# Encoder layer on one Trainium2 core: in the first feed-forward's second run, partial sums reach x by ScalarE and accumulating DMAs instead of VectorE

## The chip, the cores and the metric

The kernel runs on one core of one Trainium2 chip. The time is device microseconds of one execution. TensorE (PE in the profile) does the matmuls, ScalarE (ACT) and VectorE (DVE) the elementwise work, GpSimd (POOL) little here, and SyncE (SP) issues nearly all DMAs. PE writes its results to PSUM, eight banks of 128 x 512 f32; everything else lies in SBUF, 128 partitions wide. Each engine runs its own instructions strictly in order and waits on semaphores for the others.

## The reference, cut to what matters

One layer of an encoder, with the same weights, for two batches: a prompt of 1024 tokens and a sample of 256 tokens, model width 1024, feed-forward width 2816, all in f32:

```
x <- LN1(alpha*x + 0.5*SwiGLU_1(x))                      # the first FFN: the change is here
x <- LN2(alpha*x + W_out[ RMS(S5(x)) ; RMS(Hyena(x)) ])
x <- LN3(alpha*x + 0.5*SwiGLU_2(x))
SwiGLU(x) = (silu(x @ w_gate) * (x @ w_up)) @ w_down
```

S5 is a state-space scan that the kernel does with matmuls against tables; the tables are made from the weights on the chip. Hyena is a long convolution.

## The kernel before, in words

Each f32 matmul is done as three: both operands are split into a high part and a rest (`split`, L171 on ScalarE and L172 on VectorE), and high x high, high x rest and rest x high are summed in PSUM.

The first FFN is run twice, each time as a generator `ffn`: run `fa` takes four tiles of 128 tokens (the sample and the first two of the prompt), run `fb` the other six of the prompt. A run goes through the feed-forward width in 22 columns of 128 (`ft`). For each, `gate_up` makes gate and up in four PSUM banks (L298), silu (L306, ScalarE) and the product (L307, VectorE) give the hidden values, and these are split. Down is done for groups of columns: eighteen columns make nine groups of two, and the last four make the tenth group. For one group, `down` goes over the token tiles and over the two halves of the model width: six matmuls (L331; twelve in the last group) make one 128 x 512 partial sum in one of only two banks (`bd`), and VectorE adds it to the residual x in SBUF: L336 in the first group, which also multiplies x by alpha, L338 in all others. In `fb`, which has six tiles, a group is thus a block of 12 partial sums and 72 matmuls. After the last group's sum each tile is normalised (L239 to L245) and stored. A bank is free for the next partial sum but one when its sum has been read out.

Alongside `fb`, `weave` emits pieces of another generator, `prep`, which makes S5's tables: first in eight steps of many small VectorE operations (L421 to L426), three ScalarE operations each (L558, L561) and eight stores that ScalarE issues (L564); then 32 steps with small transposes and matmuls on PE (L589, L611, L623, L628), ScalarE copies out of PSUM (L612 and others) and stores on SP's queue (L613, L620, L637).

The generators only emit operations. A building layer fixes the order on each engine when the program is built, by priority and by a model of when each operation could start, and puts in the semaphore waits; on the chip this order stands.

Of the kernel before, what the change touches and what calls it, by code (L numbers as in the profile page):

```python
# [13 lines left out]
ALU = mybir.AluOpType  # L14
# [154 lines left out]
def split(K, src, hi, lo):  # L169

    K.nc.scalar.activation(out=hi, in_=src, func=AF.Copy)  # L171
    K.nc.vector.tensor_tensor(out=lo, in0=src, in1=hi.bitcast(F32), op=ALU.subtract)  # L172
# [37 lines left out]
def chunks_of(T):  # L210
    return [(o, min(512, T - o)) for o in range(0, T, 512)]
# [21 lines left out]
def layer_norm(K, x, g, b, eps, parts=1, done=None):  # L233

    V = K.nc.vector
    st = K.small.get()[:, 0:12].rearrange("p (a b) -> p a b", a=2)
    mv = K.small.get()
    for i in range(2):
        V.bn_stats(out=st[:, i], in_=x[:, i * 512:(i + 1) * 512])  # L239
    V.bn_aggr(out=mv[:, 0:2], in_=st)  # L240
    rsqrt(K, mv[:, 2:3], mv[:, 1:2], 1.0, eps)
    for i in range(parts):
        c = slice(i * (1024 // parts), (i + 1) * (1024 // parts))
        V.scalar_tensor_tensor(out=x[:, c], in0=x[:, c], scalar=mv[:, 0:1], in1=g[:, c], op0=ALU.subtract, op1=ALU.mult)
        V.scalar_tensor_tensor(out=x[:, c], in0=x[:, c], scalar=mv[:, 2:3], in1=b[:, c], op0=ALU.mult, op1=ALU.add)  # L245
        if done:
            done(c)


def load_row(K, dst, row):  # L250
    K.nc.sync.dma_start(out=dst, in_=row.partition_broadcast(128))


def ffn(K, NT, x, xT, wg, wu, wd, lng, lnb, cfg, done):


    nc = K.nc
    T = NT * 128
    unit, size = cfg.get("unit", 1), cfg.get("size", 2)
    chunks = chunks_of(T)  # L260
    fw = cfg.get("raw", 256)
    raw = K.ring(2, 8, fw)
    wgu = K.ring(cfg.get("wgu", 2), 2, 8, 128, dt=F32R)
    bg = Banks(K, cfg["bg"])
    bd = Banks(K, cfg["bd"])
    rawgu, rawdn, ready = {}, {}, {}
    lnv, extras = [], []

    def extra(*dims):
        extras.append(K.newr(*dims))  # L270
        return extras[-1].v

    def weights(i):

        ft, up = divmod(i, 2)
        if ft >= NFT or i in ready:
            return
        o = ft * 128 % fw
        if o == 0:
            r = raw.get()  # L280
            nc.sync.dma_start(out=r, in_=(wg, wu)[up][:, ft * 128:ft * 128 + fw].rearrange("(dt p) f -> p dt f", p=128))
            rawgu[up] = r
        ready[i] = w = wgu.get()
        with K.tc.high_priority(offset=cfg.get("ahead", 0)):
            split(K, rawgu[up][:, :, o:o + 128], w[:, 0], w[:, 1])

    def gate_up(ft):
        pss = []
        for i in (2 * ft, 2 * ft + 1):
            weights(i)  # L290
            weights(i + 1)
            w = ready.pop(i)
            pss.append([bg.get(n) for _, n in chunks])
            todo = [(d, wv, c, k) for d in range(8) for wv, ks in ((0, (0, 1)), (1, (0,))) for c in range(len(chunks)) for k in ks]
            if ft == 0:
                todo.sort(key=lambda t: t[2])
            for d, wv, c, k in todo:
                nc.tensor.matmul(pss[-1][c], lhsT=w[:, wv, d], rhs=xT.parts[k][c].at(d),  # L298
                                 start=(d == 0 and wv == 0 and k == 0), stop=(d == 7 and wv == 1))
        if ft == NFT - 1:  # L300
            raw.free()
        hv = [h.get() for h in hr] if ft < NFT - 4 + size + 1 else [extra(2, n) for _, n in chunks]
        with K.tc.high_priority(offset=cfg.get("hp", 0)):
            for c, (_, n) in enumerate(chunks):
                h = tmp.get()[:, 0:n]
                nc.scalar.activation(out=h, in_=pss[0][c], func=AF.Silu)  # L306
                nc.vector.scalar_tensor_tensor(out=h, in0=pss[1][c], scalar=0.5, in1=h, op0=ALU.mult, op1=ALU.mult)  # L307
                split(K, h, hv[c][:, 0], hv[c][:, 1])
        return hv

    def load_down(ft):
        if ft < NFT:
            rawdn[ft] = rawd.get()
            nc.sync.dma_start(out=rawdn[ft], in_=wd[ft * 128:(ft + 1) * 128, :])

    def wdown(ft):
        r = rawdn.pop(ft)
        w = wdn.get() if ft < NFT - 4 + size else extra(2, D)
        with K.tc.high_priority(offset=cfg.get("ahead", 0)):
            split(K, r, w[:, 0], w[:, 1])  # L320
        load_down(ft + len(rawd.bufs))
        return w

    def down(grp, ws, last):
        for s in range(NT):
            for dh in range(2):
                ps = bd.get(512)
                n = 0
                for h, w in zip([hs[f] for f in grp], ws):
                    for a, b in ((0, 0), (0, 1), (1, 0)):  # L330
                        nc.tensor.matmul(ps, lhsT=h[s // 4][:, a, s % 4 * 128:(s % 4 + 1) * 128], rhs=w[:, b, dh * 512:(dh + 1) * 512],  # L331
                                         start=(n == 0), stop=(n == 3 * len(grp) - 1))
                        n += 1
                xv = x.at(s)[:, dh * 512:(dh + 1) * 512]
                if grp[0] == 0:
                    nc.vector.scalar_tensor_tensor(out=xv, in0=xv, scalar=ALPHA, in1=ps, op0=ALU.mult, op1=ALU.add)  # L336
                else:
                    nc.vector.tensor_tensor(out=xv, in0=ps, in1=xv, op=ALU.add)  # L338
            if last:
                cut = cfg.get("cut") if s == NT - 1 else None  # L340
                layer_norm(K, x.at(s), lnv[0].v[:, 0], lnv[0].v[:, 1], LN_EPS, *((2, cut) if cut else ()))
                if not cut:
                    done(s)


    starts = list(range(0, NFT - 4, size))
    groups = [tuple(range(f, min(f + size, NFT - 4))) for f in starts] + [tuple(range(NFT - 4, NFT))]
    weights(0)
    yield 0.01
    rawd = K.ring(cfg.get("rawd", 1), D)  # L350
    wdn = K.ring(size, 2, D, dt=F32R)
    hr = [K.ring(size + 1, 2, n, dt=F32R) for _, n in chunks]
    tmp = K.ring(2, chunks[0][1])
    hs = {0: gate_up(0)}
    for f in range(len(rawd.bufs)):
        load_down(f)
    yield unit
    for n, grp in enumerate(groups):
        last = n == len(groups) - 1
        for f in grp:  # L360
            if f not in hs:
                hs[f] = gate_up(f)
                yield unit
        if last:
            xT.free()
            wgu.free()
            lnv.append(K.new(2, D))
            load_row(K, lnv[0].v[:, 0], lng)
            load_row(K, lnv[0].v[:, 1], lnb)
        ws = [wdown(f) for f in grp]  # L370
        if last and "tail" in cfg:
            cfg["tail"]()
        if not last:
            hs[grp[-1] + 1] = gate_up(grp[-1] + 1)
            yield unit
        down(grp, ws, last)
        yield unit * len(grp) / 2
    for b in [lnv[0], rawd, wdn, tmp] + hr + extras:
        b.free()


# [1169 lines left out]
def emit(ctx, tc, nc, A, dbg=None):  # L1551
    K = Ctx(ctx, tc, nc)
# [27 lines left out]
    def load_x(tiles):  # L1580
        x = Parts(K, len(tiles), D)
        for i, (src, s) in enumerate(tiles):
            nc.sync.dma_start(out=x.at(i), in_=src[:, s])
        return x

    def tokens(ap, nm):
        return ap.rearrange("(c s) d -> c s d", s=PARTS[nm][1])
# [7 lines left out]
    def ffn1(tiles, cfg, done=None):  # L1595

        x = load_x([(tokens(A["x_" + nm][0], nm), s) for nm, s in tiles])

        def each(i):
            nm, s = tiles[i]  # L1600
            nc.sync.dma_start(out=scr["x1_" + nm][:, s], in_=x.at(i))
            if done:
                done(x, i)

        xT = transposed(x, len(tiles), cfg["bd"])
        yield from ffn(K, len(tiles), x, xT, g("ffn1_w_gate"), g("ffn1_w_up"), g("ffn1_w_down"), g("ln1_g"), g("ln1_b"), cfg, each)
        x.free()
# [6 lines left out]
    keep, out, x1T = {}, {}, {}  # L1614
# [16 lines left out]

    fb = ffn1([("prompt", s) for s in range(2, 8)], dict(bg=(0, 1, 2, 3), bd=(4, 5), tail=to_mix, rawd=2), turn1)
    fa = ffn1([("sample", 0), ("sample", 1), ("prompt", 0), ("prompt", 1)],
              dict(bg=(0, 1), bd=(2, 3), raw=128, tail=lambda: steps(fb, 1)))
    steps(fa, 1)
# [252 lines left out]
```

## Time and profile before

| | us |
|---|---|
| median of 3 runs (lowest, highest) | 2579.18 (2578.24, 2588.45) |
| the profiled execution | 2584.32 |
| its span, first to last instruction | 2582.5 |
| PE busy | 2523.1 (98%) |
| DVE busy | 1810.0 (70%) |
| ACT busy | 812.3 (31%) |
| POOL busy | 74.7 (3%) |

All times in the rows below are of the profiled execution, counted from the start of its span. A row of a group of instructions gives their count, the busy time, the mean of one, and the idle time of the engine just before them with what ended it. ACTq and SPq are the sequencers of ScalarE and SyncE issuing DMAs. `s` is any SBUF buffer of the pool, `banks` is PSUM, `cst` a constant.

### The profile page before, as it was taken

The page shows a single profiled execution, that of the slowest core. Times are in us where ns is not written, and L with a number is a line of the kernel's source. Part 1 is how long each engine was busy: PE and PEld are TensorE (multiplying, and loading weights), DVE is VectorE, ACT ScalarE, POOL GpSimd, SP SyncE. Part 2 cuts the span into 40 slices and gives each one's busy share as a digit, 9 for nine tenths or more (in the row PEclk, how much of TensorE's full clock was granted, in tenths as well). Part 3 has the DMA queues.
Part 4 walks back from the last instruction along what each step waited for, and adds up shares of the span by engine and source line. Part 5 has one row for each costly group of instructions (what it writes and reads, how often), then busy time and mean ns, then how long its engine had stood idle before and what let it go on. Part 6 is the DMA issues. An engine that isn't in the chain of part 4 may idle for free.

```text
span 2582.5 us, 32676 instructions
## 1 busy us (share of the span) xinstructions
PE 2523.1 (98%) x12833; PEld 2112.1 (82%) x12833; DVE 1810.0 (70%) x3016; ACT 812.3 (31%) x1218; POOL 74.7 (3%) x58
## 2 busy tenths in 40 slices
PE   8999999999999999999999999999989999999998
PEld 6767887888888888788888878898768888888887
DVE  6777777568944666557896888788886556556437
ACT  5443344321322222223444313333332222223200
POOL 0000000000000000000000000000230000000001
PEclk9999999999999999999999999999999999999999
DMA  6332333533632333355566754564432223245311
GB/s 198 117 88 83 106 102 98 171 103 110 166 86 75 109 100 104 87 156 146 170 179 180 237 189 145 168 189 151 141 114 90 89 74 98 74 143 191 124 40 65
DMA packets 329073, 326.44 MB, mean 126 GB/s; under 512 B 41068, under 2 KB 285445, under 8 KB 328150
## 3 DMA queue, kind: packets, MB, share of 16 engines
q1 hardware_dynamic: 293366, 305.99, 37.5%
q10 hardware_dynamic: 35552, 18.36, 2.7%
q8 instruction: 101, 1.65, 0.3%
q14 instruction: 54, 0.44, 0.1%
HBM read 249.57 MB, written 74.46 MB: 125 GB/s over the span
## 4 chain that ended last, share of the span: by engine, by line
PE 82%; DVE 12%; DMA 3%; issue 2%; POOL 1%; ACT 1%; SPq 0%; DVEq 0%; ACTq 0%; POOLq 0%
PE banks L298 26%; PE banks L1367 16%; PE banks L331 12%; PE banks L1510 8%; PE banks L857 4%; PE banks L1238 3%; DVE s L927 3%; PE banks L774 3%; PE banks L1060 2%; DVE s L172 2%; PE banks L1201 1%; DVE s L245 1%; PE banks L1113 1%; DVE s L975 1%; DMA s<-in_ffn_w_gate_dram 1%
## 5 line engine op out<-in xcount | busy, mean ns | idle before, releaser
L298 PE MATMUL banks<-s,s 128*128 128x512 f32 (+1 forms) x4224 | 792.8, 342 | 3.3 <-ACT s L171 2.5
L298 PEld LDWEIGHTS banks<-s,s 128*128 128x128 f32 x4224 | 650.4, 190 | 99.6 <-issue 10.7
L171 ACT ACTIVATE s<-s 128x1024 fp32r<-128x1024 f32 (+3 forms) x467 | 437.8, 955 | 860.7 <-PE banks L298 239.0
L172 DVE TENSOR_TENSOR s<-s,s 128x1024 fp32r<-128x1024 f32 (+3 forms) x467 | 505.1, 1096 | 193.2 <-ACT s L171 191.0
L1367 PE MATMUL banks<-s,s 128*128 128x512 f32 x1848 | 423.4, 391 | 4.3 <-DVE s L172 3.4
L1367 PEld LDWEIGHTS banks<-s,s 128*128 128x128 f32 x1848 | 347.5, 188 | 78.7 <-DVE s L172 4.9
L331 PE MATMUL banks<-s,s 128*128 128x512 f32 x1584 | 393.0, 396 | 2.0 <-DVE s L172 1.0
L331 PEld LDWEIGHTS banks<-s,s 128*128 128x128 f32 x1584 | 291.2, 189 | 64.2 <-issue 2.1
L857 PE MATMUL banks<-s,s 128*128 128x512 f32 (+1 forms) x1152 | 238.1, 361 | 0.0
L1510 PE MATMUL banks<-s,s 128*128 128x512 f32 x704 | 216.8, 389 | 0.2 <-DVE s L172 0.2
L857 PEld LDWEIGHTS banks<-s,s 128*128 128x128 f32 x1152 | 188.3, 190 | 28.1 <-DVE s L172 0.4
L338 DVE TENSOR_TENSOR s<-banks,s 128x512 f32<-128x512 f32 x204 | 139.1, 688 | 49.1 <-PE banks L331 48.0
L1510 PEld LDWEIGHTS banks<-s,s 128*128 128x128 f32 x704 | 132.1, 188 | 28.1 <-DVE s L172 0.7
L1383 DVE TENSOR_TENSOR s<-banks,s 128x512 f32<-128x512 f32 x110 | 75.9, 690 | 106.5 <-PE banks L1367 105.7
L1510 PE MATMUL banks<-s 128*128 128x512 f32 x352 | 136.9, 389 | 0.0
L1238 PE MATMUL banks<-s,s 128*128 128x512 f32 x480 | 125.2, 409 | 3.2 <-ACT s L171 1.6
L1516 DVE TENSOR_TENSOR s<-banks,s 128x512 f32<-128x512 f32 x80 | 55.0, 690 | 97.1 <-PE banks L1510 97.1
L230 POOL TENSOR_TENSOR cst<-cst 128x1 f32<-128x1 f32 (+2 forms) x38 | 49.9, 1313 | 2496.0 <-DVE cst L229 2496.0
L1238 PEld LDWEIGHTS banks<-s,s 128*128 128x128 f32 x480 | 90.1, 192 | 23.1 <-ACT s L171 2.0
L307 DVE SCALAR_TENSOR_TENSOR s<-banks,s 128x512 f32<-128x512 f32 (+1 forms) x88 | 47.6, 554 | 84.3 <-PE banks L298 83.4
L543 DVE TENSOR_TENSOR s<-s,cst 128x288 f32<-128x288 f32 (+1 forms) x128 | 53.5, 438 | 53.5 <-PE banks L623 26.9
L676 DVE TENSOR_TENSOR s<-banks,s 128x512 f32<-128x512 f32 (+2 forms) x112 | 59.2, 552 | 44.4 <-ACT s L793 20.4
(210 smaller groups left out, 2347.8 us busy)
## 6 DMA issues: line engine op xcount, KB each, us to landing
s<-in_ffn_w_down_dram SPq DMA_DIRECT2D x88, 512.0 KB
s<-in_ffn_w_gate_dram SPq DMA_DIRECT2D x66, 512.0 KB
s<-in_ffn_w_up_dram SPq DMA_DIRECT2D x66, 512.0 KB
s<-in_ffn_w_gate_dram SPq DMA_DIRECT2D x11, 1024.0 KB
s<-in_ffn_w_up_dram SPq DMA_DIRECT2D x11, 1024.0 KB
scr_h<-s SPq DMA_DIRECT2D x22, 512.0 KB
s<-scr_h SPq DMA_DIRECT2D x22, 512.0 KB
scr_tab<-s ACTq DMA_DIRECT2D x64, 160.0 KB
```

Of the source, the lines that this page charges most:

```text
L171: K.nc.scalar.activation(out=hi, in_=src, func=AF.Copy)
L172: K.nc.vector.tensor_tensor(out=lo, in0=src, in1=hi.bitcast(F32), op=ALU.subtract)
L298: nc.tensor.matmul(pss[-1][c], lhsT=w[:, wv, d], rhs=xT.parts[k][c].at(d), start=(d == 0 and wv == 0 and k == 0), stop=(d == 7 and wv == 1))
L331: nc.tensor.matmul(ps, lhsT=h[s // 4][:, a, s % 4 * 128:(s % 4 + 1) * 128], rhs=w[:, b, dh * 512:(dh + 1) * 512], start=(n == 0), stop=(n ...
L338: nc.vector.tensor_tensor(out=xv, in0=ps, in1=xv, op=ALU.add)
L774: nc.tensor.matmul(ps, lhsT=F[kt][a].v[:, s, i], rhs=b.v[:, s], start=(n == 0), stop=(n == 3 * NT // R - 1))
L857: nc.tensor.matmul(p, lhsT=w[:, wv, d], rhs=xT[nm].parts[k][c].at(d), start=(d == 0 and wv == 0 and k == 0), stop=(d == 7 and wv == 1))
L927: TT = lambda o, a, b, op: V.tensor_tensor(out=o, in0=a, in1=b, op=op)
L1238: nc.tensor.matmul(ps, lhsT=y[s // per][a].v[:, k, ts], rhs=W[k].v[:, b, dh * 512:dh * 512 + 512], start=(k == 0 and a == 0 and b == 0), s ...
L1367: self.K.nc.tensor.matmul(ps, lhsT=w[i][:, d], rhs=x[k][:, d], start=first and m == 0, stop=m == len(todo) - 1, skip_group_check=True)
L1383: TT = lambda o, a, b: V.tensor_tensor(out=o, in0=a, in1=b, op=ALU.add)
L1510: nc.tensor.matmul(ps, lhsT=p[a].v[:, 1, o:o + 128], rhs=p[b].v[:, 0, dh * 512:dh * 512 + 512], start=m == 0, stop=m == len(todo) - 1)
```

## The change

In run `fb`, in all groups but the first and the last, a partial sum no longer goes to VectorE: ScalarE copies it from its bank into one of four staging buffers of 128 x 512 in SBUF, taken in turn, and GpSimd issues a DMA that adds the buffer to the same half tile of x. That is eight groups of 12, so 96 copies and 96 DMAs in place of 96 of L338. A staging buffer may be written again when the DMA that read it has landed. Run `fa` and the second FFN are not touched.

```diff
                 xv = x.at(s)[:, dh * 512:(dh + 1) * 512]
-                if grp[0] == 0:
+                if stage and grp[0] and not last:
+                    t = stage[0].get()
+                    nc.scalar.copy(out=t, in_=ps)
+                    nc.gpsimd.dma_start(out=xv, in_=t, accum_op=ALU.add)
+                elif grp[0] == 0:
                     nc.vector.scalar_tensor_tensor(out=xv, in0=xv, scalar=ALPHA, in1=ps, op0=ALU.mult, op1=ALU.add)
                 else:
                     nc.vector.tensor_tensor(out=xv, in0=ps, in1=xv, op=ALU.add)
...
+    stage = [K.ring(cfg["stage"], 512)] if "stage" in cfg else []
...
-    for b in [lnv[0], rawd, wdn, tmp] + hr + extras:
+    for b in [lnv[0], rawd, wdn, tmp] + stage + hr + extras:
...
-    fb = ffn1([("prompt", s) for s in range(2, 8)], dict(bg=(0, 1, 2, 3), bd=(4, 5), tail=to_mix, rawd=2), turn1)
+    fb = ffn1([("prompt", s) for s in range(2, 8)], dict(bg=(0, 1, 2, 3), bd=(4, 5), tail=to_mix, rawd=2, stage=4), turn1)
```

The new lines move all that follows by four or five: L338, L558, L561, L564, L590, L591 and L612 of before are L342, L563, L566, L569, L595, L596 and L617 of the changed program, where the new copy is L337 and the new DMA L338.

ScalarE's order at the first staged block (`fb`'s second group) before; L564 are the table stores, `s_65`, `s_66` table buffers, the L171 of `s_53` splits a gate or up weight and that of `s_55` a down weight:

```order
L171 ACTIVATE s_53_3371<-s_51_3369 128x1024
L558 COPY s_65_4322<-s_65_4322 128x4x32
L558 COPY s_66_4323<-s_66_4323 128x4x32
L564 DMA scr_tab<-s_65_4322 64x4x160
L561 ACTIVATE s_66_4323<-s_66_4323 128x640
L564 DMA scr_tab<-s_65_4322 64x4x160 x3
L564 DMA scr_tab<-s_66_4323 64x4x160 x4
L171 ACTIVATE s_55_3512<-s_54_3511 128x1024
```

The same place on ScalarE now; `s_60` and `s_61` hold the staging buffers, `s_66`, `s_67` the table buffers:

```order
L337 COPY s_60_3517<-banks 128x512 x2
L171 ACTIVATE s_53_3371<-s_51_3369 128x1024
L563 COPY s_66_4323<-s_66_4323 128x4x32
L563 COPY s_67_4324<-s_67_4324 128x4x32
L337 COPY s_61_3518<-banks 128x512
L566 ACTIVATE s_67_4324<-s_67_4324 128x640
L569 DMA scr_tab<-s_66_4323 64x4x160
L337 COPY s_61_3518<-banks 128x512
L337 COPY s_60_3517<-banks 128x512
L569 DMA scr_tab<-s_66_4323 64x4x160 x2
L337 COPY s_60_3517<-banks 128x512
L569 DMA scr_tab<-s_66_4323 64x4x160
```

The reading of the banks now stands among the table's operations, each of which waits for VectorE or for an earlier store.

ScalarE's order at the sixth staged block now; L595, L596 and L617 read small results of `prep` out of PSUM, L617 into a buffer that a store must have left:

```order
L337 COPY s_60_3517<-banks 128x512
L337 COPY s_61_3518<-banks 128x512 x2
L595 ACTIVATE s_61_3518<-banks,cst 128x128
L596 ACTIVATE s_61_3518<-banks 128x128
L617 COPY s_68_5946<-banks 128x256
L337 COPY s_60_3517<-banks 128x512 x2
L617 COPY s_68_5946<-banks 128x256
L337 COPY s_61_3518<-banks 128x512 x2
```

There too each bank's reading stands behind what was put before it. GpSimd's queue, which had only small operations of the normalisations, now holds the 96 DMAs in a row, `s_41` to `s_43` being x:

```order
L230 TENSOR_TENSOR cst<-cst 128x1 x4
L338 DMA s_41_3281<-s_60_3517 128x512 x2
L338 DMA s_41_3281<-s_61_3518 128x512 x2
L338 DMA s_42_3282<-s_60_3517 128x512 x2
L338 DMA s_42_3282<-s_61_3518 128x512 x2
L338 DMA s_43_3283<-s_60_3517 128x512 x2
```

The four L230 belong to `fa`'s normalisations; nothing else of GpSimd stands between the DMAs.

## Rows read from the trace of the kernel before

**Rows 1.** The page: engines' busy time, then the chain's shares by engine.
```profile
PE 2523.1 (98%) x12833; PEld 2112.1 (82%) x12833; DVE 1810.0 (70%) x3016; ACT 812.3 (31%) x1218; POOL 74.7 (3%) x58
...
PE 82%; DVE 12%; DMA 3%; issue 2%; POOL 1%; ACT 1%; SPq 0%; DVEq 0%; ACTq 0%; POOLq 0%
```
**Rows 2.** Windows: run `fb` whole; its staged blocks one, two, three and seven.
```profile
core 0: us, PE busy (x) PEld busy (x) DVE busy (x) ACT busy (x) POOL busy (x), PEclk, DMA share, GB/s
510.00:1070.00 560.00, 559.92 (x3052) 477.89 (x3051) 369.36 (x990) 139.01 (x267) 5.12 (x4) 1.00 0.35 102
630.00:648.00 18.00, 17.92 (x81) 14.44 (x80) 17.46 (x66) 3.33 (x7) 0.00 (x0) 1.00 0.65 172
681.00:699.00 18.00, 18.00 (x83) 14.91 (x82) 17.31 (x65) 3.67 (x7) 0.00 (x0) 1.00 0.58 158
731.00:749.00 18.00, 18.00 (x82) 14.94 (x81) 10.52 (x16) 2.59 (x4) 0.00 (x0) 1.00 0.20 61
943.00:963.00 20.00, 20.00 (x101) 16.28 (x99) 15.54 (x33) 5.26 (x13) 0.00 (x0) 1.00 0.40 118
```
**Rows 3.** Groups by line, 510 to 1070 us, different shapes apart.
```profile
L338 DVE TENSOR_TENSOR s<-banks,s 128x512 f32<-128x512 f32 x103 | 70.6, 690 | 30.4 <-PE banks L331 29.8
...
L306 ACT ACTIVATE s<-banks 128x512 f32<-128x512 f32 x22 | 12.8, 583 | 18.8 <-PE banks L298 18.8
...
L433 DVE TENSOR_TENSOR s<-s,s 128x1024 f32<-128x1024 f32 x6 | 7.3, 1220 | 0.0
...
L230 POOL TENSOR_TENSOR cst<-cst 128x1 f32<-128x1 f32 x4 | 5.1, 1279 | 527.9 <-DVE cst L229 527.9
...
L484 DVE COPY s<-s 64x128 f32<-64x128 f32 x5 | 1.1, 219 | 0.0
```
**Rows 4.** Timeline of PE, the third staged block: start, us, what.
```profile
731.13 2.94 PE L331 MATMUL banks<-s,s 128*128 128x512 f32 x12
733.92 1.44 PE L298 MATMUL banks<-s,s 128*128 128x512 f32 x7
735.19 13.82 PE L331 MATMUL banks<-s,s 128*128 128x512 f32 x60
```
**Rows 5.** Chain of waits at the end of `fb`: start, us, what.
```profile
1080.69 0.57 SPq L637
1081.27 0.04 issue
1081.31 2.45 DMA scr_mat<-s
1083.76 0.02 issue
1083.77 6.13 DMA s<-scr_x_prompt
1089.91 0.04 issue
1089.95 0.44 PE banks L221 x2
```
**Rows 6.** DMA issues, 1070 to 1096 us: sizes of those two.
```profile
s<-scr_x_prompt SPq DMA_DIRECT2D x2, 512.0 KB
scr_mat<-s SPq DMA_DIRECT2D x8, 64.0 KB
```
**Rows 7.** Timeline of ACT in the first staged block.
```profile
635.05 0.48 ACT L558 COPY s<-s 128x128 f32<-128x128 f32 x2
642.33 0.58 ACTq L564 DMA_DIRECT2D scr_tab<-s  x1
643.09 0.74 ACT L561 ACTIVATE s<-s 128x640 f32<-128x640 f32 x1 [7.56 <-DVE s L421]
643.11 4.64 ACTq L564 DMA_DIRECT2D scr_tab<-s  x7
```
**Rows 8.** Timeline of VectorE, the L338 within that wait.
```profile
636.63 0.69 DVE L338 TENSOR_TENSOR s<-banks,s 128x512 f32<-128x512 f32 x1
...
638.71 1.35 DVE L338 TENSOR_TENSOR s<-banks,s 128x512 f32<-128x512 f32 x2
...
641.20 0.69 DVE L338 TENSOR_TENSOR s<-banks,s 128x512 f32<-128x512 f32 x1
...
642.56 0.69 DVE L338 TENSOR_TENSOR s<-banks,s 128x512 f32<-128x512 f32 x1
```
**Rows 9.** Who waited for whom on ACT, 510 to 1070 us: total, times, longest.
```profile
ACT s L612 <- issue: 36.3, 10, 7.5
...
ACT s L558 <- DMA scr_tab<-s: 10.0, 2, 6.4
```
**Rows 10.** Line L612: its sequencer's waits, min/median/max ns.
```profile
L612 ACTq EVENT_SEMAPHORE  x30: 217/2304/8935, 835.5 to 1058.2; - x30
```
**Rows 11.** Who waited for whom on PE, 1030 to 1360 us.
```profile
PE banks L987 <- DVE s L927: 8.8, 7, 1.9
PE banks L221 <- DMA s<-scr_x_prompt: 4.2, 1, 4.2
PE banks L912 <- DVE s L892: 1.0, 3, 0.4
PE banks L963 <- DMA s<-scr_mat: 0.4, 2, 0.3
```

## The prediction, made before the changed kernel ran

> **What bounds the kernel now.** I read the page first: TensorE is busy for 2523.1 us of the span of 2582.5 us, and the chain that ended last runs over it for 82% and over VectorE for 12% [rows 1]. So I asked for the stage of the change alone. Run `fb` lies between about 510 and 1070 us, and there TensorE is busy for 559.92 us of 560.00 at a granted clock of 1.00, which is its higher level, 2.4 GHz; VectorE is busy for 369.36 us and ScalarE for 139.01 us [rows 2]. The reader is to see that the idle time of the bounding engine in this stage is 0.08 us. What the change takes off VectorE is therefore hidden work, and all that it can win inside the stage is 0.08 us. The question is only whether the new way out of the banks keeps TensorE waiting.
>
> The pace to be kept is read in the third staged block: 60 down matmuls in a row take 13.82 us, 0.23 us each, so a partial sum of six is made every 1.38 us [rows 4]. There are two banks: a sum must have been read out within 1.38 us of its end.
>
> **What the change removes.** 96 additions on VectorE at 690 ns [rows 3] are 66 us of its 369. They lie beside TensorE and are worth 0. What is late next, once VectorE is faster, is still TensorE.
>
> **What it adds, one part at a time.**
>
> The copy. ScalarE's silu of 128x512 out of PSUM takes 583 ns [rows 3]; I take 0.58 us for the copy. It is less than 1.38 us, so a copy that starts when its sum is ready frees its bank 0.80 us before TensorE wants it. 96 of them are 56 us more on an engine busy for 139 of 560 us. Worth 0 while ScalarE comes to them in time.
>
> The return of a staging buffer. Four buffers are taken in turn, so the fifth copy waits until the first DMA has landed. At the pace of TensorE, four sums take 5.53 us; the copy takes 0.58 of them; so a DMA may take 4.95 us from the end of its copy to its landing. Beyond that, copies five to eight are late by the excess and nine to twelve by twice the excess, less the 0.80 us of slack: a block loses 2 x excess - 0.80 us, and there are eight blocks. The trace has no accumulating DMA and none of GpSimd's, so I bound it. GpSimd's part: its smallest operation here takes 1.28 us [rows 3]; 0 is the lower end. The transfer: a store of 64 KB lands 2.45 us after its issue, and two loads of 512 KB land 6.13 us after theirs began [rows 5, 6]. A buffer is 256 KB, and adding means reading x as well, so 512 KB are read; on the line between the two rows 512 KB are 2.45 + 448 / 960 x 3.68 = 4.17 us, and 256 KB are 3.19. With GpSimd's part the bounds are 2.45 and 7.41 us, and the two points on the line are 4.47 and 5.45. I take 4.5 us to 5 us, the side of the smaller transfer, since the upper row is two transfers that together carry four times a buffer. Then the excess is at most 0.05 us, and with the slack the cost is 0. At 7.41 us the excess is 2.46 and a block loses 4.1 us, 33 us in eight blocks.
>
> The Trainium skill, page "DMA: Bandwidth & Descriptors", section "Anatomy of one DMA — SWDGE (gpsimd) path", gives a fit for DMAs that GpSimd issues: 2.0 us and the bytes over 436 GB/s. By it an estimate for 256 KB would be 2.6 us and for 512 KB read 3.2 us, and the sum would be 0 here as well; no run so far shows such a DMA.
>
> The place in ScalarE's queue. In the first two staged blocks the copies stand among the table operations, each of which waits for VectorE or for a store, and ScalarE also issues the stores. Before, nobody waited for ScalarE there: it sat 7.56 us until VectorE had made a table, and issued seven stores in 4.64 us [rows 7]. Now a copy behind such a wait holds a bank, and then TensorE. Of the 7.56 us, VectorE spent 3.45 us on five additions [rows 8] that are gone, so 4.1 us remain, and TensorE has 0.80 us of slack and, if the wait begins as a sum begins, the 1.38 us of the next sum: 1.9 us a block at the least if the wait falls between copies, 0 if it falls at a block's edge. The waits for earlier stores, up to 6.4 us [rows 9], are the upper end: 5.6 us after slack. I take 3 us for each of the two blocks, 6 us. In staged blocks five to eight two or three of the small PSUM reads (L617) stand between the copies. Before, that line's sequencer waited 30 times with a median of 2.3 us, the longest 8.9 [rows 10], and the engine sat idle for 36.3 us in ten of these waits [rows 9]. Some of them will fall between copies. 0 is the lower end; the upper is 36.3 us less ten times the slack, 28 us. I take 2 us, nearer the lower end, because most of the copies of that line stand outside the down blocks, where TensorE is at gate and up and waits for no copy. Behind a copy that waits, ScalarE's queue holds the splits of the next weights; those are wanted at the end of the block, so they cost nothing unless the block itself is late.
>
> GpSimd's queue. 96 DMAs stand in a row and before them only `fa`'s normalisations, so each is issued as its copy ends, if GpSimd needs less than 1.38 us for one; its nearest row is 1.28 us.
>
> The transfers. 25 MB written and twice that read, beside a stage whose DMA engines are busy for 0.35 of the time [rows 2]. The weights are loaded a group ahead; 0.
>
> After the stage. VectorE's order and the places of buffers move, and TensorE's order moves until about 1350 us. Between 1030 and 1360 us TensorE waits for 14.4 us [rows 11]; this can get better or worse by some microseconds. I take 0.
>
> **The sum.** 0 + 0 + 6 + 2 = +8 us on the profiled execution: 2584.3 + 8 = 2592.3. The median of the runs before lies 5.1 us below that execution, so the time to be measured is 2579.2 + 8 = 2587 us: no change that a measurement of this kernel tells, since it can tell about 0.5%, 12.9 us.
>
> **The rivals.**
>
> *The staging buffers come back too late: slower.* It decides from 4.95 us on. For it: the point on the line for 512 KB, 5.45 us, is already over, by 0.5 us (0.2 us a block, 2 us in all), and in the first two staged blocks the DMA engines are busy for 0.65 and 0.58 of the time [rows 2] with queues in which these transfers must stand. Against it: the later blocks have shares of 0.20 and 0.40. At the upper bound it costs 33 us on top of the 8: 2620 us.
>
> *ScalarE's queue costs its upper ends: slower.* 5.6 us in each of two blocks and half of the 28 us later: 25 us, 2604 us. For it: the copies really stand behind these waits; against it: the wait for VectorE shrinks as VectorE loses the additions.
>
> *VectorE holds up GpSimd: slower.* If GpSimd can write no descriptors while VectorE runs an instruction of a certain kind, a DMA waits for the end of it; the longest here is 1.22 us [rows 3]. Then 4.95 us become 6.2, a block loses 1.7 us and all 14 us, 2601 us with the 8. For it: VectorE is busy for 17.4 of 18 us in the first staged blocks. Against it: nearly all its instructions there have two tensor inputs, and its plain copies are five of 0.22 us [rows 3]. This is the rule of the Trainium skill, page "SBUF — State Buffer", sections "SBUF: two separate sides" and "A bandwidth-pool intuition that's wrong": a fp32 copy or another instruction of VectorE that uses both ports locks GpSimd out of a port that they share, it cannot write descriptors, and a DMA of 620 ns took 3100 ns beside such a copy. By the page's own condition it would hardly strike here; no run so far shows it.
>
> *The freed VectorE time shows: faster.* It can only show where TensorE waits for VectorE after the stage, and all TensorE's waits there, until the orders meet again, are 14.4 us [rows 11], of which VectorE ends 9.8. If all of them went and nothing else changed, 2565 us. Against it: those operations come after `fb` and depend on its end.
>
> **How the numbers follow.** No change by 8 us, with its own range of 2574 to 2593: 0.55. Buffers late: 0.19. ScalarE's queue at its upper ends: 0.13. VectorE against GpSimd: 0.05. Faster: 0.08. Of the first case 0.51 lies within 0.5% and 0.04 above; the three slower rivals lie above but for 0.03; the faster rival is half within. That makes faster 0.04, same 0.58, slower 0.38. The range goes from 2570, a little above the faster rival's best, to 2628, the late buffers' upper bound with another 8 us, since two of the slower rivals can come together; about a tenth is left out on either side.
>
> **What would show it.** In the profile after, 96 of VectorE's additions are gone from the stage, and TensorE's busy share of it is what tells: if TensorE's waits for the new copy (L337) in the stage are below 10 us, the forecast's steps hold. If they lie in the first two blocks and name the table's operations behind ScalarE, the term of 6 us is right in kind. If the copies' own waits name the DMAs into x, and the time from a copy's end to its buffer's next writing is over 4.95 us in all eight blocks, the first rival is right. If ScalarE's copies take much more than 0.58 us, or GpSimd more than 1.38 us for a DMA, the pace itself is broken and the prediction with it, in all eight blocks.

## The result and the profile after

The changed kernel takes 2644.48 us (median of 4 runs, 2642.06 to 2645.36) against 2579.02 us of the kernel before in the same job: a ratio of 1.0244, 95% interval 1.0219 to 1.0268, 65 us slower. The prediction was 2587 us, with a range up to 2628; it was wrong, and the time lies beyond the range.

The page after, the rows that answer to [rows 1], with the new queue's row (packets, MB, share of 16 engines' span) between them:

```profile
PE 2547.8 (96%) x12833; PEld 2122.6 (80%) x12833; DVE 1752.9 (66%) x2920; ACT 865.5 (33%) x1314; POOL 158.8 (6%) x154
...
q0 software_dynamic: 13824, 25.17, 5.5%
...
PE 64%; issue 14%; DVE 12%; DMA 4%; POOL 4%; ACT 1%; SPq 0%; POOLq 0%; DVEq 0%; ACTq 0%
```

VectorE lost 57 us of work, and TensorE, which does the same 12833 matmuls, is busy for 25 us more. To see where, take the stretch from the first staged sum to the last matmul of the next stage but one (L857 before, L862 after): the same 4201 matmuls in both. The columns are span, PE busy, granted clock, DMA share and GB/s. Before:

```profile
630.56:1414.20 783.64, 768.70 (x4201) 1.00 0.45 130
```

After:

```profile
628.88:1472.10 843.22, 793.72 (x4201) 0.97 0.60 152
```

The stretch is longer by 59.6 us of the 60.9 by which the span grew; what follows it takes 1171.3 us now and took 1168.3. Idle time grew from 14.9 to 49.5 us (34.6), busy time by 25.0, and the granted clock fell. So 58% of the stretch's loss are waits, and the rest is the same matmuls done more slowly.

Who waits for whom, 500 to 1190 us (total, times, longest), first TensorE, which before had two waits there, 6.1 us in all, both after the stage:

```profile
PE banks L331 <- ACT s L337: 28.4, 17, 6.2
PE banks L628 <- DVE s L548: 4.6, 2, 3.5
PE banks L331 <- ACT s L171: 2.6, 1, 2.6
PE banks L616 <- DVE s L548: 0.9, 1, 0.9
```

Then ScalarE, of which the copies' line is the new one:

```profile
ACT s L337 <- DMA s<-s: 52.6, 32, 5.2
ACT s L589 <- DMA s<-in_ssm_c_re_dram: 12.7, 3, 7.4
```

And VectorE, in its operations of the scan's preparation (L548 now, L543 before):

```profile
DVE s L548 <- DMA scr_mat<-s: 34.9, 5, 14.7
```

The same row before:

```profile
DVE s L543 <- DMA scr_mat<-s: 1.1, 1, 1.1
```

TensorE waits for the copy, and the copy for the adding DMA that must leave its buffer. The other rows are transfers that have nothing to do with the buffers: a small load (L589), for which ScalarE had waited 3.8 us at the longest, and stores into the scan's matrices, which VectorE hardly waited for before. They land late too.

Five of the eight staged blocks, to set beside [rows 2], where TensorE never waited and the DMA share was 0.20 to 0.65:

```profile
628.88:655.00 26.12, 24.32 (x109) 0.93 0.93 204
682.60:707.00 24.40, 20.41 (x87) 1.00 1.01 221
738.40:762.00 23.60, 19.84 (x77) 0.86 1.03 251
795.20:814.20 19.00, 16.91 (x76) 1.00 0.85 174
...
908.60:939.00 30.40, 22.62 (x93) 0.86 0.83 171
```

By this share the 16 DMA engines are nearly full while a block runs; it sums the packets' times, which overlap where it is over 1. The fourth block shows the mechanism cleanly, since nothing of the scan's preparation runs in it. ScalarE's timeline:

```profile
796.97 0.57 ACT L337 COPY s<-banks 128x512 f32<-128x512 f32 x1
...
800.91 0.59 ACT L337 COPY s<-banks 128x512 f32<-128x512 f32 x1 [0.77 <-PE banks L331]
805.04 0.59 ACT L337 COPY s<-banks 128x512 f32<-128x512 f32 x1 [3.54 <-DMA s<-s]
806.30 0.59 ACT L337 COPY s<-banks 128x512 f32<-128x512 f32 x1 [0.68 <-DMA s<-s]
807.55 0.59 ACT L337 COPY s<-banks 128x512 f32<-128x512 f32 x1 [0.66 <-DMA s<-s]
```

GpSimd's and TensorE's, the same block:

```profile
797.83 0.87 POOL L338 DMA_DIRECT2D s<-s  x1 [33.78 <-ACT s L337]
```

```profile
795.70 7.89 PE L331 MATMUL banks<-s,s 128*128 128x512 f32 x34
805.68 8.45 PE L331 MATMUL banks<-s,s 128*128 128x512 f32 x36 [2.09 <-ACT s L337]
```

The first copy ends at 797.54, and its buffer is free at 805.04: 7.5 us, where the pace allows 4.95. From then on a buffer comes back every 1.25 to 1.34 us. Everything that belongs to the engines themselves is as forecast: the copy takes 587 ns (564 to 595, x96) and GpSimd's issue of a DMA 872 ns (at most 1225, x96), both inside the 1.38 us of a sum. Only the landing is late: 3.3, 6.6 and 10.1 us (lowest, median, highest) from its issue. The reader is to see that 0.87 us on GpSimd is the issue alone; the transfer's time stands in no engine's row.

A share of 5.5% of 2643.4 us, over 96 DMAs, is 1.51 us of packet time on all 16 DMA engines for each. Since packets' times overlap, this is not a rate, and it alone does not make a landing late: the buffers just named came back faster than one in 1.38 us. What else moves at the time belongs beside it. The fourth block's transfers from 797 to 805 us, and then from 806 to 814 us (queues: packets, MB, share; issues: count, KB each, median us to landing):

```profile
q1 hardware_dynamic: 1040, 1.05, 43.7%
q0 software_dynamic: 233, 0.44, 30.4%
...
s<-in_ffn_w_up_dram SPq DMA_DIRECT2D x1, 1024.0 KB
s<-s POOLq DMA_DIRECT2D x4, 256.0 KB, 7.1
```

```profile
q0 software_dynamic: 861, 1.57, 110.5%
...
s<-s POOLq DMA_DIRECT2D x7, 256.0 KB, 4.2
```

SyncE issues the load of an up weight, 1 MB, at 797.58 us, just before the first adding DMA. The four adding DMAs beside it land after 7.1 us; those behind it have the engines to themselves, land after 4.2 us and keep the pace, and TensorE waits no more. In all eight blocks this load is issued between 1.2 us before and 3.7 us after the first adding DMA. Before the change it fell into the blocks as well, and made up nearly all of the third block's share of 0.20 (731 to 749 us):

```profile
q1 hardware_dynamic: 1045, 1.05, 19.3%
...
s<-in_ffn_w_up_dram SPq DMA_DIRECT2D x1, 1024.0 KB
```

No run moves this load; that it makes the block's first landings late is read from these times and not tested.

### The profile page after: what moved, and what is told of

Read it like the earlier page. It is cut to its first block, busy times and chain, and to the rows that moved or that the text cites. A ratio compares the mean times of both kernels' runs of the same rounds, so it can differ in the third digit from the quotient of the medians.

```text
span 2643.4 us, 32977 instructions
## 1 busy us (share of the span) xinstructions
PE 2547.8 (96%) x12833; PEld 2122.6 (80%) x12833; DVE 1752.9 (66%) x2920; ACT 865.5 (33%) x1314; POOL 158.8 (6%) x154
## 4 chain that ended last, share of the span: by engine, by line
PE 64%; issue 14%; DVE 12%; DMA 4%; POOL 4%; ACT 1%; SPq 0%; POOLq 0%; DVEq 0%; ACTq 0%
PE banks L1372 16%; PE banks L298 15%; PE banks L331 8%; PE banks L1515 8%; PE banks L862 4%; DVE s L932 3%; PE banks L779 3%; PE banks L1243 3%; POOL s L338 3%; PE banks L1065 2%; DVE s L172 2%; PE banks L1206 1%; PE banks L1118 1%; DVE s L980 1%; ACT s L171 1%
## 5 line engine op out<-in xcount | busy, mean ns | idle before, releaser
L298 PE MATMUL banks<-s,s 128*128 128x512 f32 (+1 forms) x4224 | 794.0, 342 | 1.6 <-ACT s L171 0.7
L298 PEld LDWEIGHTS banks<-s,s 128*128 128x128 f32 x4224 | 653.5, 191 | 99.2 <-issue 10.8
L171 ACT ACTIVATE s<-s 128x1024 fp32r<-128x1024 f32 (+3 forms) x467 | 439.0, 956 | 810.9 <-PE banks L298 247.6
L172 DVE TENSOR_TENSOR s<-s,s 128x1024 fp32r<-128x1024 f32 (+3 forms) x467 | 505.3, 1096 | 235.7 <-ACT s L171 233.7
L331 PE MATMUL banks<-s,s 128*128 128x512 f32 x1584 | 414.4, 407 | 33.6 <-ACT s L337 28.4
L1372 PE MATMUL banks<-s,s 128*128 128x512 f32 x1848 | 423.5, 391 | 4.4 <-DVE s L172 4.1
L862 PE MATMUL banks<-s,s 128*128 128x512 f32 (+1 forms) x1152 | 239.4, 362 | 0.0
L1515 PE MATMUL banks<-s,s 128*128 128x512 f32 x704 | 216.8, 389 | 0.0
L862 PEld LDWEIGHTS banks<-s,s 128*128 128x128 f32 x1152 | 189.2, 190 | 28.5 <-DVE s L172 0.4
L230 POOL TENSOR_TENSOR cst<-cst 128x1 f32<-128x1 f32 (+2 forms) x38 | 50.0, 1315 | 2017.7 <-DVE cst L229 2017.7
L1388 DVE TENSOR_TENSOR s<-banks,s 128x512 f32<-128x512 f32 x110 | 75.9, 690 | 106.5 <-PE banks L1372 105.7
L548 DVE TENSOR_TENSOR s<-s,cst 128x288 f32<-128x288 f32 (+1 forms) x128 | 54.1, 438 | 117.1 <-PE banks L628 41.8
L1243 PE MATMUL banks<-s,s 128*128 128x512 f32 x480 | 124.3, 406 | 4.4 <-ACT s L171 2.2
L1521 DVE TENSOR_TENSOR s<-banks,s 128x512 f32<-128x512 f32 x80 | 55.0, 690 | 97.1 <-PE banks L1515 97.1
L338 POOL DMA_DIRECT2D s<-s x96 | 84.1, 888 | 452.9 <-ACT s L337 339.7
L779 PE MATMUL banks<-s,s 128*128 128x256 f32 x624 | 89.7, 285 | 0.0
```

The lines of the kernel that those rows point to most:

```text
L338: nc.gpsimd.dma_start(out=xv, in_=t, accum_op=ALU.add)
L779: nc.tensor.matmul(ps, lhsT=F[kt][a].v[:, s, i], rhs=b.v[:, s], start=(n == 0), stop=(n == 3 * NT // R - 1))
L862: nc.tensor.matmul(p, lhsT=w[:, wv, d], rhs=xT[nm].parts[k][c].at(d), start=(d == 0 and wv == 0 and k == 0), stop=(d == 7 and wv == 1))
L1243: nc.tensor.matmul(ps, lhsT=y[s // per][a].v[:, k, ts], rhs=W[k].v[:, b, dh * 512:dh * 512 + 512], start=(k == 0 and a == 0 and b == 0), s ...
L1372: self.K.nc.tensor.matmul(ps, lhsT=w[i][:, d], rhs=x[k][:, d], start=first and m == 0, stop=m == len(todo) - 1, skip_group_check=True)
L1388: TT = lambda o, a, b: V.tensor_tensor(out=o, in0=a, in1=b, op=ALU.add)
```

## The experiments

Theory L says that TensorE pays for the buffers' late return, theory Q for what stands before the copies in ScalarE's queue. After the first four runs L was split: D holds that the adding transfers fill the DMA engines, G that GpSimd's way of issuing is slow whatever is transferred. All ratios are to the kernel before in the same job.

**Five buffers.**

```diff
-rawd=2, stage=4), turn1)
+rawd=2, stage=5), turn1)
```

> Five staging buffers instead of four, all else as changed. Theory L (the buffers come back late): a DMA lands about 6.8 us after the end of its copy; four buffers allow 4 x 1.38 - 0.58 = 4.95 us, five allow 6.33, so a block loses 2 x 0.5 - 0.8 = 0.2 us instead of 2.9, and of the 65 us lost most comes back: 2590 to 2605 us, the rest being the one wait of 6 us in ScalarE's queue and its clock. Theory Q (the copies stand behind ScalarE's other work): the buffers' number is nothing to it, 2635 to 2650 us.

2647.06 us, 1.0264 [1.0243, 1.0285]: nothing won. The wait for L337 fell from 28.4 to 14.8 us, but the median landing rose from 6.6 to 7.5 us, and the waits moved on: L628 waited for VectorE (L548) for 13.5 us in the place of 4.6. One more buffer let one more transfer stand in the same engines. As a plain latency, L is refuted.

**Two buffers.**

```diff
-rawd=2, stage=4), turn1)
+rawd=2, stage=2), turn1)
```

> Two staging buffers instead of four. Theory L: two allow 2 x 1.38 - 0.58 = 2.18 us, the excess is 4.6 us in each of five further rounds of a block, 5 x 4.6 - 0.8 = 22 us a block and 178 us in eight, and with as much again or less for the clock: 2760 to 2930 us. Theory Q: 2640 to 2660 us.

2667.24 us, 1.0336 [1.0318, 1.0354], between both expectations. With two in flight the landing's median is 4.4 us, and L337 keeps TensorE waiting for 47.1 us in 29 waits. But the number in flight explains little of a block's first landings: in the fourth block the two beside the up weight's load (807 to 815 us) land as late as four did, and those behind it (816 to 830 us) after 3.3 us, where four took 4.2:

```profile
s<-s POOLq DMA_DIRECT2D x2, 256.0 KB, 7.1
```

```profile
s<-s POOLq DMA_DIRECT2D x7, 256.0 KB, 3.3
```

**ScalarE copies, VectorE adds, no DMA.**

```diff
-                    nc.gpsimd.dma_start(out=xv, in_=t, accum_op=ALU.add)
+                    nc.vector.tensor_tensor(out=xv, in0=t, in1=xv, op=ALU.add)
```

> ScalarE copies to the four staging buffers as changed, but VectorE adds them to x instead of a DMA. A buffer is back about 1 us after its copy. Theory L: TensorE's waits go but for what ScalarE's queue costs, 2580 to 2600 us. Theory Q: the copies stand where they stood, 2635 to 2650 us.

2587.18 us, 1.0025 [1.0015, 1.0035], and 1.4 us of waits for L337. The copies stand in ScalarE's queue as in the changed kernel; that place, with all else that the detour brings, costs some 6 us. Q is refuted as the cause of the 65.

**VectorE copies, adding DMAs as changed.**

```diff
-                    nc.scalar.copy(out=t, in_=ps)
+                    nc.vector.tensor_copy(out=t, in_=ps)
```

> VectorE copies to the four staging buffers instead of ScalarE, the accumulating DMAs as changed. Theory L: the buffers are as late as before and the copy waits on VectorE, 2625 to 2650 us. Theory Q: ScalarE holds no bank any more, 2578 to 2590 us.

2639.73 us, 1.0233 [1.0214, 1.0252]. Nearly the whole loss is there without ScalarE: it goes with the DMA.

**GpSimd's DMAs without the adding.**

```diff
-                    nc.gpsimd.dma_start(out=xv, in_=t, accum_op=ALU.add)
+                    nc.gpsimd.dma_start(out=xv, in_=t)
```

> GpSimd's 96 DMAs copy the staging buffer over x and don't add to it (the sum is left out, so the values of x are others; instructions, sizes, queue and waits stay). Theory D (the adding transfers fill the 16 DMA engines: about 170 ns per 2 KB packet, 1.5 us of all 16 per DMA, over the 1.38 us pace of the sums): a packet then costs about 84 ns as a plain one of before, the queue's share halves from 5.5% to about 2.8%, the median landing falls from 6.6 to below 4.5 us, TensorE's waits for L337 fall from 28 us to below 8, and the time is 2585 to 2605 us. Theory G (what costs is GpSimd's way of issuing: its descriptors and their latency, whatever the transfer does): the landing stays at 6 us or more and the time stays at 2630 to 2650 us. Theory Q (the copies stand behind ScalarE's other work): 2635 to 2650 us.

2603.27 us, 1.0087 [1.0069, 1.0104]. The queue, the issue and the waits, TensorE's then ScalarE's:

```profile
q0 software_dynamic: 7680, 25.17, 2.6%
```

```profile
L338 POOL DMA_DIRECT2D s<-s x96: 546/546/719, 631.1 to 1029.0; - x96
...
DMA to landing us min/median/max: 2.2/3.9/7.1
```

```profile
PE banks L331 <- ACT s L337: 6.8, 7, 1.3
```

```profile
ACT s L337 <- DMA s<-s: 25.2, 22, 3.0
```

The same bytes take 2.6% in the place of 5.5%, that is 0.70 us of packet time on all engines for a DMA in the place of 1.51, and land in 3.9 us. Here too those beside the up weight's load land later (in the fourth block a median of 5.2 us for the four from 782 to 788.5 us) than those behind it (2.3 us, 789.5 to 798.4). 41 of the 65 us are gone. D is borne out in what it says of the adding's price, not in that the adding alone overfills the engines; G is refuted.

**The plain copy issued by SyncE.**

```diff
-                    nc.gpsimd.dma_start(out=xv, in_=t, accum_op=ALU.add)
+                    nc.sync.dma_start(out=xv, in_=t)
```

> The same plain copy over x, the sum left out, issued by SyncE in the place of GpSimd. Theory D: as with GpSimd, landings of 3 to 4 us, 2585 to 2605 us, unless the weight loads that stand behind these DMAs in SyncE's queue come late, which would show as TensorE's waits for gate, up or down weights and not for L337. Theory G: without GpSimd's issuing the landing is 2.5 to 3.5 us and the time 2580 to 2595 us; it differs from D in that the run with GpSimd's plain DMAs stays at 2630 or more. Theory Q: 2635 to 2650 us.

2596.34 us, 1.0058 [1.0041, 1.0075]. GpSimd's issuing is worth some 7 us at most, and the intervals of the two runs touch; the adding is worth 41.

**Every second sum, two buffers.**

```diff
-                if stage and grp[0] and not last:
+                if stage and grp[0] and not last and dh == 1:
...
-rawd=2, stage=4), turn1)
+rawd=2, stage=2), turn1)
```

> Only the second of each row block's two sums goes by staging buffer and adding DMA, the first is added by VectorE as before; two staging buffers in the place of four, so that a DMA has the same 4.95 us between its copy's end and the buffer's next use, at half the DMA load (48 DMAs, one per 2.76 us). Theory D: landings fall to 4 to 5 us, the share of the DMA engines in the blocks to 0.4 to 0.8, TensorE's waits for L337 to below 8 us, 2582 to 2600 us. Theory G (a landing of 6.6 us is the way's latency): each buffer is late by 1.6 us, six DMAs a block on two buffers lose about 2.5 us a block, 20 us with as much again by a lower clock: 2605 to 2630 us. Theory Q: half the copies, 2605 to 2620 us.

2607.38 us, 1.0096 [1.0074, 1.0118]: above D's range and in those of G and Q. What was expected of the mechanism came: the landing's median is 4.0 us, the DMA share 0.66 and 0.64 in the third and fourth block, and L337 makes TensorE wait for 3.9 us. What D missed is that VectorE now reads every other bank, and its additions (L342) keep TensorE waiting for 7.5 us. Half the load costs less than half.

**Two buffers of double width.**

```diff
-                    t = stage[0].get()
-                    nc.scalar.copy(out=t, in_=ps)
-                    nc.gpsimd.dma_start(out=xv, in_=t, accum_op=ALU.add)
+                    t = stage[0].get() if dh == 0 else t
+                    nc.scalar.copy(out=t[:, dh * 512:(dh + 1) * 512], in_=ps)
+                    if dh == 1:
+                        nc.gpsimd.dma_start(out=x.at(s), in_=t, accum_op=ALU.add)
...
-    stage = [K.ring(cfg["stage"], 512)] if "stage" in cfg else []
+    stage = [K.ring(cfg["stage"] // 2, D)] if "stage" in cfg else []
```

> Two staging buffers of 1024 columns in the place of four of 512: ScalarE fills both halves and one DMA of 512 KB adds them, 48 DMAs of 4 KB a partition. The same bytes. If the cost in the DMA engines is by the packet, theirs is halved: the queue's share falls from 5.5% to about 2.8%; if it is by the byte, it stays at 5 to 6%. A buffer must be back 3.6 us after its second copy, less than the 4.95 of before, and nothing shown lands sooner than 3.3 us, so theory D by the byte expects more waits for L337 than 28 us and 2645 to 2690 us; by the packet 2610 to 2650 us.

2648.02 us (two runs), 1.0259 [1.0238, 1.028], which lies in both ranges. The queue's row tells them apart:

```profile
q0 software_dynamic: 6912, 25.17, 5.0%
```

Half the packets, nearly the same share: the adding costs mostly by the byte, 2.76 us of packet time on all engines for 512 KB, 1.38 for 256.

**The DMA load without a wait for a buffer.** VectorE adds from the bank as before, and the DMAs add the new x to spare buffers.

```diff
-                    t = stage[0].get()
-                    nc.scalar.copy(out=t, in_=ps)
-                    nc.gpsimd.dma_start(out=xv, in_=t, accum_op=ALU.add)
+                    nc.vector.tensor_tensor(out=xv, in0=ps, in1=xv, op=ALU.add)
+                    t = stage[0].get()
+                    nc.gpsimd.dma_start(out=t, in_=xv, accum_op=ALU.add)
...
+    for b in stage:
+        for t in b.bufs:
+            nc.gpsimd.memset(t.v if hasattr(t, "v") else t, 0.0)
```

> VectorE adds every sum to x as before the change, and no copy is made; 96 adding DMAs of the same size, by GpSimd, add the new x to four spare buffers that nobody reads. TensorE's banks therefore wait for no DMA, and the load of the DMA engines stays that of the changed kernel (about 5.5% for this queue, a share of 0.85 to 1.03 in the blocks). It asks which part of the 65 us comes from the staging buffers' return and which from other transfers that the load delays. Theory D1 (the copy's wait for a buffer is what TensorE pays for, with the lower clock behind it): TensorE's waits in the stage fall from 40 us to below 8 and the time is 2580 to 2600 us. Theory D2 (the load delays the loads and stores of the weights and of the scan's preparation, and these cost as much): waits that name L548, L589, L171 or L172, 15 to 25 us, 2610 to 2640 us.

2627.63 us, 1.0184 [1.0168, 1.0199], in D2's range, though the waits are named otherwise than it said. TensorE's waits (500 to 1190 us), and VectorE's timeline before the longest (L551 is the preparation's L548, L336 the addition):

```profile
PE banks L331 <- DVE s L336: 26.3, 5, 12.2
```

```profile
989.33 0.46 DVE L551 TENSOR_TENSOR s<-s,cst 128x288 f32<-128x288 f32 x1 [13.03 <-DMA scr_mat<-s]
989.70 0.68 DVE L336 TENSOR_TENSOR s<-banks,s 128x512 f32<-128x512 f32 x1
```

TensorE's wait of 12.2 us ends at 990.44, when this addition has emptied a bank. The load alone, then, makes the stores of the scan's preparation land late (SyncE also issues them more slowly: eight take it 8.87 us from 965.79, and took 4.92 before the change, from 948.31); VectorE stands for them, and its additions stand behind. In the first block TensorE never waits, at a DMA share of 0.99: full DMA engines hurt only through who waits for a landing. How this part and the buffers' part add up in the changed kernel is not separated by it, since there ScalarE reads the banks and not VectorE.

**Idle time without DMAs, first attempt.** In the kernel in which VectorE adds, three of a block's twelve copies are made five times.

```diff
-                    nc.scalar.copy(out=t, in_=ps)
+                    for _ in range(5 if s % 2 and dh else 1):
+                        nc.scalar.copy(out=t, in_=ps)
```

> No DMA at all: ScalarE copies to staging buffers and VectorE adds them to x, and in three of the twelve sums of a block ScalarE makes its copy five times over, 2.9 us in the place of 0.58, so that TensorE waits some 1.5 us for the bank, 24 times, about 36 us in the stage, which is the idle time that it has in the changed kernel. It asks what idle time alone does to TensorE's clock. Theory C (the clock is lowered after TensorE has waited, whatever it waited for): the same matmuls take 15 to 30 us more between the waits, a granted clock of 0.95 to 0.97 in the stage, 2635 to 2660 us. Theory N (the busy time that grew is a mark of the DMA load and not of the waits): busy time as before, clock 1.00, 2587 and 36, that is 2615 to 2628 us.

2591.78 us, 1.0048 [1.0032, 1.0065], and no answer: TensorE waited for 0.8 us in all. With single copies the block was 72 down matmuls in a row (16.51 us from 729.35). Now:

```profile
737.30 2.25 PE L298 MATMUL banks<-s,s 128*128 128x256 f32 x12
739.39 1.54 PE L331 MATMUL banks<-s,s 128*128 128x512 f32 x6
740.77 1.20 PE L298 MATMUL banks<-s,s 128*128 128x256 f32 x6
741.81 2.88 PE L331 MATMUL banks<-s,s 128*128 128x512 f32 x12
```

The longer copies are known when the order is made, and gate and up matmuls (L298) were put between the sums. A delay that the order foresees was hidden almost whole; the landing of the changed kernel is one that it did not foresee.

**Idle time without added DMA load, second attempt.** VectorE adds; a DMA of 128 x 4 bytes holds each of two buffers until it lands.

```diff
-                    nc.gpsimd.dma_start(out=xv, in_=t, accum_op=ALU.add)
+                    nc.vector.tensor_tensor(out=xv, in0=t, in1=xv, op=ALU.add)
+                    nc.gpsimd.dma_start(out=tiny.get()[:, 0:1], in_=t[:, 0:1])
...
+    tiny = K.ring(4, 1) if stage else None
...
-    for b in [lnv[0], rawd, wdn, tmp] + stage + hr + extras:
+    for b in [lnv[0], rawd, wdn, tmp] + stage + ([tiny] if tiny else []) + hr + extras:
...
-rawd=2, stage=4), turn1)
+rawd=2, stage=2), turn1)
```

> The slowed copies of the run before were foreseen when the order was made, and TensorE hardly waited; this one makes it wait without a load on the DMA engines. ScalarE copies, VectorE adds the staging buffer to x, and GpSimd's DMA takes one column of the staging buffer (128 x 4 bytes) to a spare place, so that the buffer must wait for a landing; two buffers. At the pace of the sums a landing may come 2.2 us after the copy's end; I expect 2.5 to 3.3, that is 0.3 to 1.1 us late for each pair of sums, some 15 to 45 us of waits for L337 in the stage. Theory C (the clock is lowered where TensorE has waited, whatever it waited for): the same matmuls take 0.4 to 1 us more for each us of waiting, at a granted clock below 0.98 in the stage. Theory N (the added busy time comes with the DMA load): the busy time of the stage as in the kernel before, clock 1.00, and the time is 2587 and the waits, no more.

2607.58 us, 1.0105 [1.0085, 1.0125]. The same stretch as above, then a wait in the third block:

```profile
627.63:1431.90 804.27, 775.24 (x4202) 0.99 0.44 127
```

```profile
740.54 4.61 PE L331 MATMUL banks<-s,s 128*128 128x512 f32 x12 [1.82 <-ACT s L337]
745.22 2.90 PE L331 MATMUL banks<-s,s 128*128 128x512 f32 x12
```

At a DMA share no higher than before the change, idle time is 14.1 us more than before it and busy time 6.5 us more. Behind the wait twelve matmuls take 4.61 us, the next twelve 2.90. Theory C is borne out in kind: the clock falls behind waits, with no more load on the DMA engines than before. It does so behind some of them: the granted clock is 0.91 in the 20 us around the waits at 740, 794 and 908 us, and 1.00 around one of 2.36 us at 688. The clock of the whole stretch, 0.99, is above the 0.98 expected, and the size is not shown. By the sums it would be 0.46 us for each us of idle time, but the first attempt, which hardly waited and whose clock was 1.00, also has 5.1 us more busy time than the kernel before the change, its gate and up matmuls likewise put between the sums:

```profile
628.20:1418.30 790.10, 773.83 (x4202) 1.00 0.44 130
```

In the changed kernel it is 25.0 us of busy time for 34.6 of idle time at a clock of 0.97.

No variant beats the kernel before, and none could by much: in this stage it waits for nothing [rows 2].

## Why the prediction was wrong

*What bounds the kernel, and VectorE's relief at 0: right.* With 57 us less work on VectorE nothing became faster; no row of the stretch shows a gain.

*The copy and GpSimd's issue: right.* 0.587 us for 0.58, and 0.872 us, under the 1.28 us of the nearest row and well under 1.38.

*The return of a staging buffer and, under it, the transfers at 0: the step that failed.* "I take 4.5 us to 5 us, the side of the smaller transfer [...] and with the slack the cost is 0." In every block the first copy that waits for a buffer finds it only 6.0 to 8.9 us after that buffer's last copy ended. The bounds were 2.45 and 7.41 us; the upper one was nearer, and was itself too low. Yet 4.5 us fits an adding DMA that has the engines to itself: 4.2 us from its issue, some 4.5 from its copy's end. What was wrong, as far as the times show it, is the step beside it, *the transfers*: "The weights are loaded a group ahead; 0." That load, 1 MB for an up weight, falls into each block about where the first adding DMAs are issued, and beside it they land after 7.1 us in the fourth block, with their packets' time twice a plain copy's (1.51 and 0.70 us). I compared 25 MB with a mean share of 0.35 over the whole stage; the step needed what moves at the same time in a block. The adding's price could not be read from the trace of before, the load's place could.

*The formula for a block.* In the fourth block the excess is 2.55 us; 2 x excess - 0.80 gives 4.3, and TensorE waited for 2.1. Once the first buffer is back, the others follow at 1.26 us, under the pace, and no second excess comes, since by then the load is over. The two errors went opposite ways. Taken with the right landing, the first rival was right: it named the place, all eight blocks, and its test, the copies' waits for DMAs into x.

*ScalarE's queue, +8: near in size, by luck.* The kernel in which VectorE adds is 6.4 us over the one before by the ratio (8 by the medians), but the waits that I priced are not what it pays: the copies keep TensorE waiting once, for 1.4 us, in the second block. The 36.3 us of L612's idle time that I took for its waits stand in [rows 9] as "issue", time for which the row names no wait. In the changed kernel one more wait in that queue did cost, and for another reason: the copies of the sixth block stood behind L589, which waited 7.38 us for a small load (before the change 3.8 us at the longest), and TensorE waited 6.16 us for them.

*VectorE holding up GpSimd: no sign of it.* GpSimd's issue takes 872 ns in the median and 1225 at the most, beside VectorE at work.

*After the stage, 0: right.* What follows the stretch is 3.0 us longer.

*A term that was missing.* A wait of TensorE was priced at its length. In the changed kernel's third block, after 3.76 us of waiting, 36 matmuls take 10.96 us, 0.30 us each, where [rows 4] show 0.23; over the stretch it is 25 us on top of 34.6, a few of which may be the matmuls' other order and not the clock. The granted clock of 0.86 in that block is a mean of its two levels, 1.2 and 2.4 GHz. Even at the upper bound my rival had 33 us of waits and no such term.

The Trainium skill, page "DMA: Bandwidth & Descriptors", section "Anatomy of one DMA — SWDGE (gpsimd) path", gives 2.0 us and the bytes over 436 GB/s, by which my estimates were 2.6 and 3.2 us. The plain DMA's lowest landing is 2.2 us and its median 3.9; the adding one's are 3.3 and 6.6. The fit is near the undisturbed transfer and has no term for the adding or for others in flight; the measurement decides.

What the runs show of the 65 us, by the medians: 41 go when the DMAs stop adding, 16 more when there is no DMA, and about 8 stay with the copies on ScalarE alone. What stays open is what moving the up weight's load would give back, and the split of the 41 between the buffers' own return and the late transfers of others: in the changed kernel the copies' waits for buffers carry some 22 of the 28.4 us that L337 cost TensorE and the sixth block's late load the rest, but with the load alone, in another order of reading, 48 us are lost too.

## What to carry to other kernels

Before moving work from an idle-looking engine to a DMA, look at what else the DMA engines carry in the very stretch in which it will be issued; a share over the whole stage hides it. Here a load at the head of each block, which had cost nothing before, met transfers whose landing the bounding engine now waited for, and a fifth buffer only let the waits move on. Price a wait of TensorE above its length, since behind some waits its matmuls run at the lower clock for a while. Work taken off an engine that hides behind TensorE was worth nothing, so this change could only lose.

## What the hardware showed that was not expected

- A DMA that adds takes 1.51 us of packet time on all 16 DMA engines for 256 KB from SBUF to SBUF, a plain one 0.70; GpSimd needs 872 ns to issue the first and 546 for the second, and the queue holds 144 packets for it in the place of 80.
- The adding is paid mostly by the byte: with 512 KB in one DMA and half as many packets, 1.38 us for 256 KB.
- Landings went with what else moved more than with the number in flight: in the fourth block adding DMAs land after 7.1 us beside a load of 1 MB, with two buffers and with four, and after 3.3 and 4.2 us behind it.
- A wait of 1.8 us of TensorE, in a stretch with no more DMA load than before, was followed by twelve matmuls at 0.38 us each and then twelve at 0.24.
